# Forgetting attention by two pairs of heads at a time, its tail in another order, five moves in the order of the latent attention, and shifted buffers

## The chip, the cores and the metric

The kernel runs on one core of one Trainium2 chip. A core has a matrix engine (TensorE, PE), a vector engine (VectorE, DVE), a scalar engine (ScalarE, ACT), a general engine (GpSimd, POOL) and SyncE (SP), whose queue issues the DMA transfers here. Engines run their own streams in order and wait for one another through semaphores. The metric is the device time of one execution in microseconds (us).

## What is computed

The reference is a trunk of two layers on 256 tokens of width 1024. Each layer is a half-step SwiGLU network (FFN, inner width 2816), a mixer, a second FFN and a gated input embedding, each followed by a layer norm over `ALPHA*x + delta`. The mixer of layer 0 is forgetting attention (FoX, 16 heads of 64), that of layer 1 latent attention (MLA, 16 heads of 128 + 64 rotary columns), whose shared keys and values come from the residual stream between the layers.

```python
def swiglu(x, w_in, w_out):
    h = x @ w_in
    gate, up = h[..., :D_FF], h[..., D_FF:]
    return (jax.nn.silu(gate) * up) @ w_out

def fox_mixer(x, w_in, b_f, w_o):
    h = x @ w_in                      # q, k, v and 16 forget gates
    ...
    cum = jnp.cumsum(jax.nn.log_sigmoid(f_logit), axis=1).transpose(0, 2, 1)
    s = jnp.einsum('bqhd,bkhd->bhqk', qb, k) * scale + cb[:, :, :, None] - cum[:, :, None, :]
    # causal softmax over k in blocks of 128 queries, times v, then @ w_o

def mla_mixer(x, w_dq, q_norm, w_uq, w_o, k_nope, k_rope, v, cos, sin):
    c_q = rms_norm(x @ w_dq, q_norm)
    q = jnp.einsum('bsc,chd->bshd', c_q, w_uq)
    s = (jnp.einsum('bqhd,bkhd->bhqk', qn, k_nope) + jnp.einsum('bqhr,bkr->bhqk', qr, k_rope)) * scale
    # causal softmax, times the shared v, then @ w_o
```

All is float32. The kernel writes each float32 operand as the sum of two float32r numbers, hi and lo, and each product as three matmuls: hi*hi, hi*lo, lo*hi.

## The kernel before

**Weights.** They stream through three `raw` buffers of 1 MB by DMAs on SP's queue. A class `Stream` cuts each group into units and splits every unit: ACT copies it to hi (`L193`, `L201`), DVE subtracts to get lo (`L194`, `L205`). A split goes to a home: ten slots `hl`, and four further buffers `ota`, `otb`, `qk` and `fs` while they are lent to it. An ordinary split issues both halves at once; `ahead` issues the ACT half alone, `later` the DVE half that is left, `split_now` is the two together, and `fill(n)` splits until the n next units are ready. `use` hands a unit to matmuls; `pump`, called between matmuls, splits when estimated times of the engines allow it, unless `hold` is set.

**Order.** A recorder runs the whole program once to learn the order in which units are used. Then the program runs for good under a manual schedule: each engine gets its instructions as the code writes them. In the FoX mixer this is a loop over pairs of heads, in the MLA mixer the table `ORDER`, whose words name steps: `gen` (keys and queries of a head), `QK`, `sm` (softmax), `div`, `T` (transposes of the probabilities P into PT), `AV`, `O h t` (output product of head h for half t of the tokens), and `f n`, `a` and `l` for `fill`, `ahead` and `later`.

**FoX.** Per pair j of heads: `gen_k` and `gen_q` are 24 matmuls each (`h<-xT,hl`, 128x256), evicted to hi and lo by ACT and DVE. `QK(j)` has 14 matmuls into two banks of `y`: two that lay down the sum of the gates (`y<-negc,sel`) and twelve of keys by queries (`y<-qk`), each on 64 of the 128 rows, one head on the upper, the other on the lower half. `softmax(j)` adds the mask and takes the least on DVE (`L1033`, ISA in the order), corrects it by the gates (`L1040`, `L1041`, tile `tt`), takes exponentials on ACT (`L1045`), reciprocals on DVE (`L1052`, tile `su`) and divides on POOL (`L1055`). `T(j)` transposes P in six matmuls (`L1070`, `L493`) and evicts to PT, `AV(j)` is six matmuls 512 wide, evicted into `ota` or `otb` (`L1096`, `L1099`), and O(k, t) is six matmuls that add up the output (`y<-hl,ota` or `otb`). A step of the loop runs, on PE, QK(j), gen_q(j+1), AV(j-1), gen_k(j+2), T(j).

PSUM has eight banks in named rings: `y` has four, `h` and `tr` two each.

**Shared keys and values.** They are produced inside the first FFN of layer 1 (`kv`), whose h products begin with the first half of the tokens; `XT(1)` transposes the second half into `xT`, evicted in turn by ACT (`L498`) and DVE (`L499`).

## Time and profile before

| what | us |
|---|---|
| median of 3 runs (lowest, highest) | 1075.26 (1074.89, 1076.74) |
| profiled execution | 1074.41 |
| its span | 1072.3 |
| busy PE, DVE, ACT, POOL | 1061.1, 721.2, 543.9, 60.0 |
| HBM traffic over the span | 185 GB/s |

The granted clock of TensorE was 0.999. Rows of a timeline give the start in us, the busy time, the engine, the line, the operation, `out<-in`, the rows and columns of TensorE used, the shape, the count of like instructions that follow each other, and in brackets the idle time of the engine just before with the instruction that ended it. The end of a matmul is modelled, and one matmul starts before the one ahead ends; so waits of PE are best read from start to start. Rows of groups give busy time, mean ns of one, and idle time of the engine just before them.

### The profile page before, as it was taken

How to read it: one execution, taken by the hardware profiler on the slowest of the kernel's cores; microseconds unless marked ns; L12 is line 12 of the kernel's file. 1: busy time of each engine (PE TensorE's matmuls, PEld its weight loads, DVE VectorE, ACT ScalarE, POOL GpSimd, SP SyncE). 2: the span in 40 equal slices, each digit the busy share in tenths (PEclk: the TensorE clock that was granted, in tenths of full speed). 3: DMA queues.
4: the chain of work that ended last, by engine and by line, in shares of the span. 5: the costliest groups of instructions: out<-in, count | busy, mean ns of one | idle time of the engine just before them, and what ended most of it. 6: DMA issues, size and time to landing. Idle time of an engine off the chain costs nothing.

```text
span 1072.3 us, 17527 instructions
## 1 busy us (share of the span) xinstructions
PE 1061.1 (99%) x7236; PEld 971.9 (91%) x7236; DVE 721.2 (67%) x1053; ACT 543.9 (51%) x805; POOL 60.0 (6%) x94
## 2 busy tenths in 40 slices
PE   9999999999999999999999999999999999999997
PEld 9989998999889999998899999989899789898986
DVE  6775545788897545548966454578887886454566
ACT  6654433667645434444555453436675466354431
POOL 0000000223200000000320000000000000000000
PEclk9999999999999999999999999999999999999999
DMA  7886642543348655354477554423334568555502
GB/s 281 342 294 224 233 160 96 200 177 119 124 176 298 231 192 189 142 201 150 175 274 263 180 192 181 153 75 108 135 139 157 193 234 313 175 208 186 190 7 79
DMA packets 33091, 199.58 MB, mean 186 GB/s; under 512 B 3698, under 2 KB 5490, under 8 KB 12148
## 3 DMA queue, kind: packets, MB, share of 16 engines
q1 hardware_dynamic: 33012, 198.47, 51.5%
q8 instruction: 57, 0.93, 0.3%
q14 instruction: 22, 0.18, 0.1%
HBM read 197.40 MB, written 1.05 MB: 185 GB/s over the span
## 4 chain that ended last, share of the span: by engine, by line
PE 88%; DVE 7%; ACT 2%; issue 1%; POOL 1%; DMA 0%; DVEq 0%; SPq 0%; POOLq 0%; ACTq 0%
PE y L489 32%; PE h L489 31%; PE tr L489 22%; DVE hl L194 2%; PE tr L493 2%; ACT P L1434 1%; DVE PT L499 1%; ACT hl L193 0%; DVE tr L1429 0%; DVE x L569 0%; DVE hl L205 0%; PE h L493 0%; DVE qk L499 0%; DVE x L550 0%; DVE st L551 0%
## 5 line engine op out<-in xcount | busy, mean ns | idle before, releaser
L194 DVE TENSOR_TENSOR hl<-raw,hl 128x1024 fp32r<-128x1024 f32 (+3 forms) x263 | 309.2, 1194 | 148.3 <-ACT hl L193 147.4
L193 ACT ACTIVATE hl<-raw 128x1024 fp32r<-128x1024 f32 (+3 forms) x263 | 266.1, 1032 | 185.3 <-PE y L489 97.0
L489 PE MATMUL h<-xT,hl 128*128 128x256 f32 x1560 | 187.1, 279 | 0.3 <-DVE hl L233 0.2
L489 PE MATMUL y<-hl,g 128*128 128x512 f32 x792 | 185.7, 390 | 0.0
L489 PEld LDWEIGHTS h<-xT,hl 128*128 128x128 f32 x1560 | 182.8, 189 | 2.2 <-ACT xT L498 0.6
L489 PE MATMUL tr<-xT,hl 128*128 128x256 f32 x1512 | 176.6, 277 | 0.0
L489 PEld LDWEIGHTS tr<-xT,hl 128*128 128x128 f32 x1512 | 174.2, 188 | 0.5
L489 PEld LDWEIGHTS y<-hl,g 128*128 128x128 f32 x792 | 147.5, 188 | 29.8
L489 PE MATMUL h<-hl,xT 128*128 128x512 f32 (+2 forms) x300 | 67.8, 374 | 0.4 <-DVE xT L499 0.4
L489 PE MATMUL y<-hl,xT 128*128 128x512 f32 (+3 forms) x348 | 64.2, 334 | 0.0
L489 PEld LDWEIGHTS h<-hl,xT 128*128 128x128 f32 x300 | 53.2, 188 | 10.7 <-DVE xT L499 0.9
L489 PEld LDWEIGHTS y<-hl,xT 128*128 128x128 f32 x348 | 53.5, 188 | 6.3 <-ACT xT L498 0.4
L561 POOL TENSOR_TENSOR rs<-ve,mhalf 128x1 f32<-128x1 f32 x16 | 15.1, 942 | 627.9 <-DVE ve L560 627.9
L499 DVE TENSOR_TENSOR g<-P,g 128x512 fp32r<-128x512 f32 x38 | 26.3, 692 | 26.5 <-ACT g L498 26.5
L489 PE MATMUL y<-hl,otb 128*128 128x512 f32 x168 | 43.1, 397 | 0.2 <-DVE otb L1099 0.2
L498 ACT ACTIVATE xT<-tr 128x512 fp32r<-128x512 f32 x28 | 16.2, 597 | 48.2 <-PE tr L493 48.2
L498 ACT ACTIVATE g<-P 128x512 fp32r<-128x512 f32 x38 | 24.0, 632 | 32.8 <-DVE P L678 32.8
L194 DVE TENSOR_TENSOR otb<-raw,otb 128x1024 fp32r<-128x1024 f32 (+1 forms) x21 | 25.3, 1204 | 17.5 <-ACT otb L193 17.5
L194 DVE TENSOR_TENSOR qk<-raw,qk 128x1024 fp32r<-128x1024 f32 (+2 forms) x22 | 26.6, 1210 | 15.0 <-ACT qk L193 15.0
L489 PEld LDWEIGHTS y<-hl,otb 128*128 128x128 f32 x168 | 30.1, 188 | 6.1 <-DVE otb L1099 0.6
L193 ACT ACTIVATE otb<-raw 128x1024 fp32r<-128x1024 f32 (+1 forms) x21 | 21.8, 1039 | 19.7 <-PE y L489 10.8
L677 ACT ACTIVATE P<-tr 128x512 f32<-128x512 f32 x20 | 12.0, 599 | 38.0 <-PE tr L489 38.0
(264 smaller groups left out, 1420.4 us busy)
## 6 DMA issues: line engine op xcount, KB each, us to landing
raw<-in_ffn_in_dram SPq DMA_DIRECT2D x85, 1024.0 KB, 5.0
raw<-in_ffn_out_dram SPq DMA_DIRECT2D x44, 1024.0 KB, 4.9
raw<-in_pg_dram SPq DMA_DIRECT2D x8, 1024.0 KB, 4.8
raw<-in_mo_dram SPq DMA_DIRECT2D x8, 1024.0 KB, 4.7
raw<-in_kq_dram SPq DMA_DIRECT2D x8, 640.0 KB, 4.0
gb<-in_ln_g_dram SPq DMA_DIRECT2D x8, 512.0 KB, 5.8
gb<-in_ln_b_dram SPq DMA_DIRECT2D x8, 512.0 KB, 6.7
raw<-in_fk_dram SPq DMA_DIRECT2D x4, 1024.0 KB, 5.0
```

The source lines that it names most:

```text
L193: nc.scalar.activation(hi, src, AF.Copy)
L194: nc.vector.tensor_tensor(lo, src, hi.bitcast(F32), op=ALU.subtract)
L489: self.nc.tensor.matmul(out, lhsT, rhs, start=start, stop=stop)
L493: self.nc.tensor.transpose(out, in_, self.ident)
L498: self.nc.scalar.activation(hi, src, AF.Copy)
L499: self.nc.vector.tensor_tensor(lo, src, hi.bitcast(F32), op=ALU.subtract)
L561: nc.gpsimd.tensor_tensor(rs, ve, self.mhalf, op=ALU.pow)
L677: nc.scalar.activation(gt, ps[0], AF.Silu)
L1434: nc.scalar.activation(P[:, c0:c1], b[:, c0:c1], AF.Exp, bias=nm[:, q : q + 1], scale=-1.0, accum_out=su[:, q : q + 1],)
```

## The change

**The FoX loop takes two pairs of heads at a time.** Two QK blocks follow one another and fill all four `y` banks. `softmax` falls into `least` (DVE), `exps` (ACT) and `divide` (DVE and POOL), issued at different places. The correction by the gates and the reciprocals are made for both heads of a pair at once (128x4). AV goes into a bank of `h`, AV(5) into `tr`. Generation of the second pair, `gen_k(1)` and `gen_q(1)`, stands ahead of the transposes of the gates. Three `split_now` stand in the second half of a pair of pairs, two of them back to back.

On PE, the step of pair 1 in the loop before (`hl_...` are weight units, `g_...` the values):

```order
L489 MATMUL y<-negc,sel 128x384 x2
L489 MATMUL y<-qk 128x128 x2
L489 MATMUL y<-qk 128x256 x2
L489 MATMUL y<-qk 128x128 x2
L489 MATMUL y<-qk 128x256 x2
L489 MATMUL y<-qk 128x128 x2
L489 MATMUL y<-qk 128x256 x2
L489 MATMUL h<-xT,hl_2108 128x256 x24
L489 MATMUL y<-PT,g_1954 128x512 x3
L489 MATMUL y<-PT,g_2156 128x2x128 x3
L489 MATMUL h<-xT,hl_2082 128x256 x24
L1070 MATMUL tr<-ident,P 128x128 x4
```

And in the loop of the change, from the last matmuls of QK 2 on:

```order
L490 MATMUL y<-qk 128x256 x2
L490 MATMUL y<-negc,sel 128x384 x2
L490 MATMUL y<-qk 128x128 x2
L490 MATMUL y<-qk 128x256 x2
L490 MATMUL y<-qk 128x128 x2
L490 MATMUL y<-qk 128x256 x2
L490 MATMUL y<-qk 128x128 x2
L490 MATMUL y<-qk 128x256 x2
L490 MATMUL h<-PT,g_1956 128x512 x3
L490 MATMUL h<-PT,g_2158 128x2x128 x3
L490 MATMUL h<-xT,hl_2155 128x256 x24
L490 MATMUL h<-xT,hl_2232 128x256 x24
```

The next QK block follows the first directly, and AV of the pair before stands behind both, where a generation (24 matmuls) stood between QK and AV.

On DVE, the end of one step before, from the reciprocals of pair 1 (two rows in one) to PT:

```order
L1052 RECIPROCAL su<-su 128x2 x2
L205 TENSOR_TENSOR hl_2373<-raw,hl_2373 128x1024
L499 TENSOR_TENSOR qk<-h,qk 128x256
L1099 TENSOR_TENSOR ota<-y,ota 64x256 x2
L205 TENSOR_TENSOR fs<-raw,fs 128x1024
L499 TENSOR_TENSOR qk<-h,qk 128x256
L499 TENSOR_TENSOR PT<-tr,PT 128x512
L499 TENSOR_TENSOR PT<-tr,PT 128x256
```

And for pairs 2 and 3 in the change, from the reciprocals of pair 2 (the first row) and of pair 3 to PT of pair 2:

```order
L1071 RECIPROCAL su<-su 128x4
L206 TENSOR_TENSOR hl_2588<-raw,hl_2588 128x1024
L500 TENSOR_TENSOR qk<-h,qk 128x256
L1071 RECIPROCAL su<-su 128x4
L206 TENSOR_TENSOR hl_2669<-raw,hl_2669 128x1024
L206 TENSOR_TENSOR hl_2674<-raw,hl_2674 128x1024
L500 TENSOR_TENSOR qk<-h,qk 128x256
L500 TENSOR_TENSOR PT<-tr,PT 128x512
L500 TENSOR_TENSOR PT<-tr,PT 128x256
```

Where one split followed both reciprocals, one now follows that of the first pair, and two in a row that of the second.

**The FoX tail** runs QK 6, QK 7, AV 5, O 0 to O 4 of the first half of the tokens, T 6, O 5, the matmuls of AV 6, T 7, the evictions of AV 6, O 0 of the second half, AV 7, O 6, O 1 of the second half, O 7. Before, O 6 stood ahead of AV 7. SP issues three more weight loads ahead of those of the norm's factors (`gb`), and one split moves behind the layer norm.

**`S.stop`** names a unit that `pump` may not split: in the `kv` FFN, unit 2 of the third product, until `XT(1)` has been issued. On DVE the split now stands behind the two evictions into `xT`.

**The table of the MLA mixer** has four places changed. `l` and a fill move from ahead of QK 4 and softmax 4 to behind them; O 5 0 moves ahead of AV 6; AV 12 moves ahead of gen 15; and a fill ahead of softmax 15 is dropped, with one `f 2` for two `f 1` behind it. On DVE, around softmax 15 before (ISA is the masked least, `nm` its result):

```order
L499 TENSOR_TENSOR PT<-tr,PT 128x384
L194 TENSOR_TENSOR hl_8425<-raw,hl_8425 128x1024
L1429 ISA tr,nm<-tr,mask 128x128
L1429 ISA nm 128x1
L1429 ISA tr,nm<-tr,mask 128x256
L1429 ISA nm 128x1
L1443 RECIPROCAL su<-su 128x2
L1446 TENSOR_SCALAR P<-P,su 128x128
L1446 TENSOR_SCALAR P<-P,su 128x256
```

And in the change:

```order
L500 TENSOR_TENSOR PT<-tr,PT 128x384
L1466 ISA tr,nm<-tr,mask 128x128
L1466 ISA nm 128x1
L1466 ISA tr,nm<-tr,mask 128x256
L1466 ISA nm 128x1
L195 TENSOR_TENSOR hl_8416<-raw,hl_8416 128x1024
L1480 RECIPROCAL su<-su 128x2
L1483 TENSOR_SCALAR P<-P,su 128x128
L1483 TENSOR_SCALAR P<-P,su 128x256
```

The split has moved from ahead of the softmax to between its least and its reciprocal.

**Buffers.** Two unused tiles of 192 and 64 bytes per partition stand around the first `gb`, so that it and all that is allocated behind it lie 192 or 256 bytes higher; slices of the shared keys in `fs` start 192 and 256 bytes later.

```diff
@@ -54,23 +54,23 @@
...
-    "l", "O 1 0", "O 1 1", "AV 2", "f 4", "a", "f 3", "gen 5", "T 3", "f 4", "l", "QK 4", "sm 4", "f 1", "f 1",
+    "l", "O 1 0", "O 1 1", "AV 2", "f 4", "a", "f 3", "gen 5", "T 3", "f 4", "QK 4", "sm 4", "l", "f 1",
...
-    "QK 7", "sm 7", "f 4", "gen 8", "div 7 0", "zs 1 1", "l", "zU 0 1", "f 4", "gen 9", "f 4", "AV 6", "f 2",
-    "O 5 0", "zU 1 0", "QK 8", "a", "T 7", "sm 8", "f 1", "O 5 1", "div 8 0", "f 3", "O 6 0", "f 4", "f 1",
+    "QK 7", "sm 7", "f 4", "gen 8", "div 7 0", "zs 1 1", "l", "zU 0 1", "f 4", "gen 9", "f 4", "O 5 0", "AV 6",
+    "f 2", "zU 1 0", "QK 8", "a", "T 7", "sm 8", "f 1", "O 5 1", "div 8 0", "f 3", "O 6 0", "f 4", "f 1",
...
@@ -138,6 +138,7 @@
         self.hold = False
         self.rest = None
         self.at = 0
+        self.stop = None
 
     def load(self, n=NRAW):
         while self.loaded < len(self.groups) and self.loaded < self.done + n:
@@ -284,7 +285,7 @@
 
     def pump(self):
 
-        if self.ready == len(self.order) or not self.slots or self.hold:
+        if self.ready == len(self.order) or not self.slots or self.hold or self.order[self.ready] == self.stop:
             return
         arrival = self.arrives.get(group_of(self.order[self.ready]), 1e12)
         if arrival <= self.pe_t + 500 and max(self.act_t, self.dve_t) <= self.pe_t + SLACK_NS:
@@ -538,7 +539,12 @@
                 self.S.pump()
 
     def load_gb(self, li, i):
+        first = (li, i) == (0, 0)
+        if first:
+            self.tl([128, 48], F32, "gap0", 1)
         self.gb = self.tl([128, 2, D], F32, "gb", 1)
+        if first:
+            self.tl([128, 16], F32, "gap1", 1)
         if not self.rec:
             self.dma(self.gb[:, 0, :], pbcast(self.a["ln_g"][li, i], D))
             self.dma(self.gb[:, 1, :], pbcast(self.a["ln_b"][li, i], D))
@@ -702,7 +708,13 @@
             first()
         else:
             H(0, 0, sweeps=SW_H00)
-            H(1, 0, HAT, lambda: self.XT(1), SW_H10)
+            S.stop = ("win", li, which, 2, 0) if kv else None
+
+            def other():
+                self.XT(1)
+                S.stop = None
+
+            H(1, 0, HAT, other, SW_H10)
             if kv:
                 self.kv_down(1)
             H(0, 1, sweeps=SW_H01)
@@ -989,17 +1001,17 @@
         qk = self.own([128, 2, 2, 512], F32R, "qk")
         OT = [self.own([128, 4, 2, 256], F32R, tag) for tag in ("ota", "otb")]
 
-        def gen(j, key, c0, at={}, hold=False):
+        def gen(j, key, c0, hold):
             ps = self.bank("h")
-            ws((key, j), ps[:, 0:256], at, hold)
+            ws((key, j), ps[:, 0:256], hold=hold)
             o = qk[:, j % 2]
             self.parts(o[:, 0, c0 : c0 + 256], o[:, 1, c0 : c0 + 256], ps[:, 0:256])
 
         def gen_k(j):
-            gen(j, "fk", 256, {0: S.split_now} if j >= 2 else {}, j >= 2)
+            gen(j, "fk", 256, j >= 2)
 
         def gen_q(j):
-            gen(j, "fq", 0, {}, j >= 2)
+            gen(j, "fq", 0, j >= 2)
 
         def QK(j, ring):
             sb = [self.bank(ring) for _ in range(2)]
@@ -1020,14 +1032,12 @@
                         )
             st[j] = sb
 
-        def softmax(j):
+        seg = ((0, 128), (128, 384))
+
+        def least(j):
             sb = st[j]
             nm = self.tl([128, 4], F32, "nm", 2)
             tt = self.tl([128, 4], F32, "tt", 2)
-            su = self.tl([128, 4], F32, "su", 2)
-            pair = self.tl([128, 768], F32, "P", 2)
-            P = [pair[:, 384 * s : 384 * s + 384] for s in range(2)]
-            seg = ((0, 128), (128, 384))
             for s in range(2):
                 for q, (c0, c1) in enumerate(seg):
                     nc.vector.tensor_tensor_reduce(
@@ -1035,10 +1045,17 @@
                         op0=ALU.add, op1=ALU.min, scale=-0.125, scalar=3.0e38,
                         accum_out=nm[:, 2 * s + q : 2 * s + q + 1],
                     )
-                c2 = cq[:, 2 * j + s, :]
-                i = slice(2 * s, 2 * s + 2)
-                nc.vector.tensor_tensor(tt[:, i], nm[:, i], c2, op=ALU.subtract)
-                nc.vector.tensor_tensor(tt[:, i], tt[:, i], c2, op=ALU.add)
+            c2 = cq[:, 2 * j : 2 * j + 2, :].rearrange("p h t -> p (h t)")
+            nc.vector.tensor_tensor(tt, nm, c2, op=ALU.subtract)
+            nc.vector.tensor_tensor(tt, tt, c2, op=ALU.add)
+            self.S.busy(dve=1400)
+            st[j] = sb, tt
+
+        def exps(j):
+            sb, tt = st[j]
+            su = self.tl([128, 4], F32, "su", 2)
+            pair = self.tl([128, 768], F32, "P", 2)
+            P = [pair[:, 384 * s : 384 * s + 384] for s in range(2)]
             for s in range(2):
                 for q, (c0, c1) in enumerate(seg):
                     i = 2 * s + q
@@ -1046,19 +1063,18 @@
                         P[s][:, c0:c1], sb[s][:, c0:c1], AF.Exp, bias=tt[:, i : i + 1], scale=-1.0,
                         accum_out=su[:, i : i + 1],
                     )
-            self.S.busy(act=1800, dve=1400)
-
-            def divide(s):
-                nc.vector.reciprocal(su[:, 2 * s : 2 * s + 2], su[:, 2 * s : 2 * s + 2])
+            self.S.busy(act=1800)
+            st[j] = P, su
+
+        def divide(j):
+            P, su = st[j]
+            nc.vector.reciprocal(su, su)
+            for s in range(2):
                 for q, (c0, c1) in enumerate(seg):
                     i = 2 * s + q
                     nc.gpsimd.tensor_scalar(
                         P[s][:, c0:c1], P[s][:, c0:c1], su[:, i : i + 1], 1.0, op0=ALU.mult, op1=ALU.mult
                     )
-
-            divide(0)
-            divide(1)
-            S.later()
             st[j] = P
 
         def T(j):
@@ -1077,9 +1093,9 @@
             self.parts(o[:, 0, 512:768], o[:, 1, 512:768], b1[:, 0:256])
             PT[j] = o
 
-        def AV(j):
+        def AV(j, what=None):
             o = PT.pop(j)
-            ps = self.bank("y" if j < 6 else "tr")
+            ps = self.bank("h" if j != 5 else "tr")
             n, c = j // 4, 128 * (j % 4)
             strided = ps.rearrange("p (s c) -> p s c", s=2)[:, :, 128:256]
             for m, (i, jj) in enumerate(((0, 0), (0, 1), (1, 0))):
@@ -1089,6 +1105,8 @@
                     strided, v[1, n][:, i, c : c + 128],
                     o[:, jj, 512:768].rearrange("p (s c) -> p s c", s=2), False, m == 2,
                 )
+            if what:
+                what()
             ot = OT[j // 4][:, j % 4]
             self.S.busy(act=700, dve=600)
             for s in range(2):
@@ -1116,41 +1134,60 @@
                     lambda i: w[:, i, 512 * n : 512 * n + 512], k == 0, k == 7,
                 )
 
-        for j in range(8):
-            if j == 2:
+        gen_k(1)
+        gen_q(1)
+        self.flush()
+        gates_transpose()
+        S.lend("fs")
+        S.hold = True
+        for a in range(0, 6, 2):
+            if a == 2:
                 self.load_gb(li, 1)
-            S.hold = j >= 1
-            if j < 7:
-                gen_k(j + 1)
-            else:
-                O(0, 0)
-                O(1, 0)
-            if j == 0:
-                self.flush()
-                gates_transpose()
-                S.lend("fs")
-            if j >= 1:
-                T(j - 1)
-                if j < 7:
-                    S.ahead()
-            QK(j, "y" if j < 7 else "h")
-            softmax(j)
-            if j < 7:
-                gen_q(j + 1)
-            else:
-                O(2, 0)
-                S.split_now()
-                O(3, 0)
-            if j >= 1:
-                AV(j - 1)
+            QK(a, "y")
+            QK(a + 1, "y")
+            least(a)
+            if a:
+                AV(a - 1)
+            exps(a)
+            S.ahead()
+            least(a + 1)
+            gen_k(a + 2)
+            exps(a + 1)
+            divide(a)
+            S.later()
+            gen_q(a + 2)
+            divide(a + 1)
+            S.split_now()
+            S.split_now()
+            gen_k(a + 3)
+            T(a)
+            S.split_now()
+            gen_q(a + 3)
+            AV(a)
+            T(a + 1)
+        QK(6, "y")
+        QK(7, "h")
+        least(6)
+        AV(5)
+        exps(6)
+        least(7)
+        S.lend("qk")
+        exps(7)
+        divide(6)
+        divide(7)
+        for k in range(2):
+            O(k, 0)
+        S.split_now()
+        for k in range(2, 5):
+            O(k, 0)
+        T(6)
+        S.split_now()
+        O(5, 0)
+        AV(6, lambda: T(7))
+        O(0, 1)
         S.hold = False
-        S.lend("qk")
-        O(4, 0)
-        O(5, 0)
-        T(7)
+        AV(7)
         O(6, 0)
-        O(0, 1)
-        AV(7)
         O(1, 1)
         O(7, 0)
         self.ln(0, y[0], ALPHA, LN_EPS)
@@ -1205,8 +1242,8 @@
     def kv_transpose_rope(self):
         nc = self.nc
         kvt = self.kvt = self.own([128, 2048], F32R, "fs")
-        self.ckv = kvt[:, 0:1024].rearrange("p (i c) -> p i c", i=2)
-        self.kr = kvt[:, 1024:1792].rearrange("p (i c) -> p i c", i=3)
+        self.ckv = kvt[:, 48:1072].rearrange("p (i c) -> p i c", i=2)
+        self.kr = kvt[:, 1088:1856].rearrange("p (i c) -> p i c", i=3)
         b = self.bank("tr")
         for t in range(2):
             self.transpose(b[:, 128 * t : 128 * t + 128], self.kvtok[:, t, 256:384])
```

10 rows, old and new, of the table ORDER are left out of this document.

## The prediction

> **What bounds the kernel now.** I read the page first, then the timeline of TensorE (PE) for what follows another late, then the engines that feed it at those places.
>
> ```profile
> PE 1061.1 (99%) x7236; PEld 971.9 (91%) x7236; DVE 721.2 (67%) x1053; ACT 543.9 (51%) x805; POOL 60.0 (6%) x94
> 228.38:262.55 34.17, 34.17 (x298) 32.47 (x298) 29.05 (x88) 24.16 (x65) 10.18 (x16) 1.00 0.42 155
> ```
>
> PE is busy 1061.1 of 1072.3 us. The second row is the windows view over four steps of the forgetting-attention loop (PE, PEld, DVE, ACT, POOL busy): PE has no gap in 34.17 us, DVE is at 29.05, 85%. The change keeps the 7236 matmuls. So there are two sources of gain alone: matmuls that start closer together, and the short holes where PE waits for DVE. One step of the loop, then part of a QK block by itself:
>
> ```profile
> 222.06 5.73 PE L489 MATMUL h<-xT,hl 128*128 128x256 f32 x48
> 227.63 0.60 PE L1070 MATMUL tr<-ident,P 128*128 128x128 f32 x4
> ...
> 228.38 0.45 PE L489 MATMUL y<-negc,sel 64*128 64x384 f32 x2
> 228.67 0.85 PE L489 MATMUL y<-qk 64*128 64x128 f32 x12
> 229.44 3.01 PE L489 MATMUL h<-xT,hl 128*128 128x256 f32 x24
> 232.30 1.21 PE L489 MATMUL y<-PT,g 128*128 128x512 f32 x6
> 233.34 3.00 PE L489 MATMUL h<-xT,hl 128*128 128x256 f32 x24
> 236.18 0.60 PE L1070 MATMUL tr<-ident,P 128*128 128x128 f32 x4
> 236.62 0.38 PE L493 MATMUL tr<-ident,P 128*128 128x128 f32 x2
> 236.93 0.44 PE L489 MATMUL y<-negc,sel 64*128 64x384 f32 x2
> ...
> 246.03 0.40 PE L489 MATMUL y<-qk 64*128 64x256 f32 x4
> 246.21 0.39 PE L489 MATMUL y<-qk 64*128 64x128 f32 x4
> 246.27 0.33 PE L489 MATMUL y<-qk 64*128 64x256 f32 x2
> 246.53 0.39 PE L489 MATMUL h<-xT,hl 128*128 128x256 f32 x1
> ```
>
> A step is 236.93 - 228.38 = 8.55 us, start to start. The QK block works on half the rows (64*128), and each change between it and full-row work costs. Going in: four transposes take 0.44 (236.18 to 236.62), two take 0.31 instead of 0.22 when QK follows, +0.09. Going out: 24 matmuls behind a QK take 2.86 (229.44 to 232.30), while 48 took 5.57 (222.06 to 227.63), so 24 without it take 2.71, +0.15. The last pair of 256-wide QK matmuls takes 0.26 (246.27 to 246.53), the one before 0.18 (246.03 to 246.21), +0.08. Together 0.32 us for each lone block.
>
> **1. QK in pairs.** Eight lone blocks become four of two; four times in and out go: 4 x 0.32 = -1.28. Against it: 24 generating matmuls behind AV take 2.84 (233.34 to 236.18), 0.13 more than 2.71. Five groups stand behind AV before; in the new order it is three each for the pairs at 2 and 4, six, +0.13. The inner block's first two matmuls (0.29, 228.38 to 228.67) may also start faster: at the pace of the 0.18 for 256 columns, 384 would take 0.27, so almost nothing is to be had there. If the last-pair and exit costs turn out to belong to every block, only the entry is saved, 4 x 0.09 = 0.36. I take -1.15, between -0.2 and -1.4. The merged tt operations, reciprocals and the split softmax are DVE work beside a busy PE: nothing, as long as DVE's 15% of slack covers it.
>
> **2. The tail.** Here one hole of PE:
>
> ```profile
> 294.00 1.20 PE L489 MATMUL y<-hl,otb 128*128 128x512 f32 x4 [0.19 <-DVE otb L1099]
> ```
>
> The idle in the bracket counts from the modelled end of the matmul before. Undisturbed matmuls start 0.16 before that end (229.44 + 3.01 = 232.45 against 232.30), so a wait seen start to start is the bracket plus 0.16: here 0.35. O of pair 7 waits for the DVE eviction of AV 7. Before, O 1 alone stands between AV 7 and O 7; in the change O 6 and O 1 do, six matmuls more. I take the hole as gone, -0.4 with its restart, between 0 and -0.5. T(7)'s evictions, now issued behind AV 6's matmuls, and the three fo loads that SP issues ahead of gb have several us of O before their readers: nothing. One split fewer is made before the layer norm and one more behind it, with other work of PE in front of its reader: nothing, at most the 1.2 us of a DVE split (row in part 5). AV now shares the banks of the generation; each is emptied behind a block of 24 matmuls, so I see no wait in that.
>
> **3. S.stop in the shared-KV stage.**
>
> ```profile
> 533.79 1.73 PE L489 MATMUL h<-hl,xT 128*128 128x320 f32 x10 [0.39 <-DVE xT L499]
> 529.44 3.69 DVE L194 TENSOR_TENSOR hl<-raw,hl 128x1024 fp32r<-128x1024 f32 x3
> 533.06 1.28 DVE L499 TENSOR_TENSOR xT<-tr,xT 128x512 fp32r<-128x512 f32 x2
> ```
>
> PE waits 0.39 + 0.16 = 0.55 for the xT parts, which DVE starts right when three splits end at 533.13. With the third behind xT they come 1.2 us earlier, more than the wait. The held split's reader comes after another group of matmuls. -0.55, between -0.2 (the wait turns to ACT's half of xT) and -0.65.
>
> **4. The table of the latent attention.**
>
> ```profile
> 765.88 0.61 PE L493 MATMUL tr<-ident,P 128*128 128x128 f32 x3 [0.16 <-DVE P L1446]
> 762.26 1.21 DVE L205 TENSOR_TENSOR hl<-raw,hl 128x1024 fp32r<-128x1024 f32 x1
> 763.39 0.29 DVE L1429 CUSTOM_DVE_ANT_0 tr<-tr,mask 128x128 f32<-128x128 f32 x1
> ...
> 783.92 1.24 PE L489 MATMUL h<-gb,hl 128*128 128x256 f32 x9
> 785.27 0.91 PE L489 MATMUL h<-PT,g 128*128 128x256 f32 x6
> 786.01 1.59 PE L489 MATMUL y<-hl,otb 128*128 128x512 f32 x6
> ...
> 825.60 0.51 PE L493 MATMUL tr<-ident,P 128*128 128x128 f32 x3
> 826.23 1.82 PE L489 MATMUL y<-hl,ota 128*128 128x512 f32 x6
> ...
> 836.81 0.61 PE L493 MATMUL tr<-ident,P 128*128 128x128 f32 x3 [0.38 <-DVE P L1446]
> 832.23 0.56 DVE L499 TENSOR_TENSOR PT<-tr,PT 128x384 fp32r<-128x384 f32 x1 [0.72 <-ACT PT L498]
> 833.18 1.22 DVE L194 TENSOR_TENSOR hl<-raw,hl 128x1024 fp32r<-128x1024 f32 x1 [0.39 <-ACT hl L193]
> 834.32 0.29 DVE L1429 CUSTOM_DVE_ANT_0 tr<-tr,mask 128x128 f32<-128x128 f32 x1
> 836.17 0.17 DVE L1443 RECIPROCAL su<-su 128x2 f32<-128x2 f32 x1 [0.98 <-ACT P L1434]
> ```
>
> T 4 waits 0.16 + 0.16 = 0.32 behind a softmax that DVE begins at 763.39 because a split runs first; with "l" behind "sm 4" the softmax starts up to 1.2 earlier: -0.32. AV 6 waits 785.27 - 783.92 - (1.24 - 0.16) = 0.27; O 5 0, a block like the six at 786.01 (1.59 - 0.16 = 1.43 us), now stands ahead of it: -0.27. O 12 0 waits 826.23 - 825.60 - (0.51 - 0.16) = 0.28 for AV 12's eviction, and its six take longer by the second half; AV 12 one generation earlier saves up to 0.6, of which AV 13, now nearer to its own PT, gives back about half: -0.3. The fourth move is a loss by its place: the split at 833.18 leaves the front of softmax 15, but its ACT half now follows the exponentials and its DVE half stands ahead of the reciprocal. From softmax to reciprocal it is 836.17 - 834.32 = 1.85 us; begun at 832.8, where DVE ends the PT row, the exponentials are done at 834.6, ACT's half of a split (1.03, row below) at 835.7, DVE's 1.22 at 836.9. The reciprocal comes 0.7 late, and T 15, which waits already (0.38 + 0.16), with it; DVE's evictions behind it slip too, so AV 15 gives little back. I take +0.6, between 0 and +1.1 (ACT's and DVE's halves half covered, or nothing of the earlier start realised). Sum of the table -0.3, between -1.2 and +0.6.
>
> **5. Homes.**
>
> ```profile
> L194 DVE TENSOR_TENSOR hl<-raw,hl 128x1024 fp32r<-128x1024 f32 (+3 forms) x263 | 309.2, 1194 | 148.3 <-ACT hl L193 147.4
> L193 ACT ACTIVATE hl<-raw 128x1024 fp32r<-128x1024 f32 (+3 forms) x263 | 266.1, 1032 | 185.3 <-PE y L489 97.0
> L194 DVE TENSOR_TENSOR qk<-raw,qk 128x1024 fp32r<-128x1024 f32 (+2 forms) x22 | 26.6, 1210 | 15.0 <-ACT qk L193 15.0
> ```
>
> The buffers move by 192, 64 or 256 bytes. The same split takes 1194 ns into the ten hl homes and 1210 into the qk home, quite another place, so I cost the move at nothing. If these 16 ns were an effect of the address and fell on each of the 285 splits of the two rows, it would be 4.6 us of DVE, with either sign, and DVE is mostly off the path.
> The Trainium skill says, in SBUF — State Buffer, Specifications (TRN2), that cachelines are 16 bytes; all three shifts are whole lines. No run here shows it.
>
> **Sum.** -1.15 - 0.4 - 0.55 - 0.3 = -2.4. The profiled execution, 1074.41 (span 1072.3 and 2.1 around it), would become 1072.0. The median of the three runs, 1075.26, lies 0.85 above it; I forecast against the median: **1072.9 us**. About 0.2% (2.15 us) is what a measurement tells from no change, so the edge of faster is 1073.1.
>
> **Rivals.** (a) *POOL is shut out, in every pair.* The rows:
>
> ```profile
> 258.18 0.82 POOL L1055 TENSOR_SCALAR P<-P,su 128x128 f32<-128x128 f32 x2 [5.73 <-DVE su L1052]
> 259.27 1.72 POOL L1055 TENSOR_SCALAR P<-P,su 128x128 f32<-128x128 f32 x2 [0.27 <-DVE su L1052]
> ...
> 259.10 1.20 DVE L205 TENSOR_TENSOR hl<-raw,hl 128x1024 fp32r<-128x1024 f32 x1
> ...
> 529.70 2.37 POOL L1193 TENSOR_SCALAR PT<-PT,rs 128x256 f32<-128x256 f32 x1
> ```
>
> Two POOL divisions take 0.82, but 1.72 when a DVE split runs beside them; at 529.70 one took 2.37 through the splits at 529.44. The change puts two splits back to back right behind the reciprocal of pair a+1, while POOL is still at pair a's four divisions. From the reciprocal they need 0.27 (the bracket at 259.27), 1.72 for the first two beside a split and 0.41 (0.82 / 2) for the third: the fourth starts after 2.4 us. The second reciprocal, and the splits behind it, come one generation later, after 2.71 to 2.84. The point that decides is this margin of 0.3 to 0.4; it is less at the first pair, whose softmax has no AV in front of the generation that follows, so that its reciprocal comes late. A fourth division that misses it ends 1.9 us late (2.37 - 0.48), and T(a) on PE with it. In three pairs +5.7, so -2.4 + 5.7 = +3.3, 1078.6, slower; chance 18%. For it: DVE is 85% full, so reciprocals drift late. Against it: in two of the three pairs nothing in these rows takes up the margin.
> The Trainium skill's SBUF — State Buffer, Who interferes with whom, speaks against the change: a DVE instruction with two SBUF inputs and a GpSimd one that reads SBUF hold a shared pair of ports exclusively, and the loser blocks for the whole instruction. By that rule, this trace agrees (1.72 against 0.82).
> (b) *Only the first pair misses:* -2.4 + 1.9 = -0.5, 1074.8, no change that can be told; 20%.
> (c) *QK costs stay with each block,* (entry only saved, and the six slow groups): -0.2 in place of -1.15: -1.45, 1073.8, no change; 14%.
> The forecast's case has 48%: as it lies only 0.2 below the edge, 3 of these may end in no change, while (c) may end below the edge by as much if the table gives more. So faster 0.47, no change 0.34 (20 + 14), slower 0.19.
>
> **Range.** Low: every term at its far end, -1.4 - 0.5 - 0.65 - 1.2 = -3.75, 1071.5, and 0.9, the distance between the profiled run and the median, below it: 1070.6. High: (a) in two pairs, -2.4 + 3.8 = +1.4, and the same 0.9: 1077.5; (a) in full lies outside. The forecast's case alone: 1071.5 to 1073.4.
>
> **What would show it.** In the changed profile: QK 6 to QK 7 and the pairs as 24 + 4 narrow matmuls without a full-row one between; a pair's period near 2 x 8.55 - 0.3 = 16.8 us; no releaser at T 4, the kv group, O 7 or AV 6; T 15 with a bracket larger than 0.38. What would make it wrong: T(0), T(2) or T(4) with a bracket that names POOL; AV(a-1) waiting for DVE's PT; or all stages longer at once, which would be the homes.

## The result, and the profile after

The changed kernel takes 1070.53 us (median of 5, 1070.12 to 1071.00); the kernel before, on the same chip, 1074.89 (1074.74 to 1076.74). The ratio is 0.9951, with a 95% interval of 0.994 to 0.9961: half a per cent less, clear of the noise. I had forecast 1072.9 with a range from 1070.6. The direction was right. The gain was 4.4 us where I had 2.4, and the time lies just below the range.

The profiled executions took 1074.41 (span 1072.3) and 1070.54 (span 1068.8). Since TensorE (PE) is the bound in both, the start of the same matmul in both traces tells what each stretch gained. Rows of PE's timeline before, then after: a matmul ahead of the FoX loop, the first long group of the FFN behind it, the first transposes ahead of the MLA mixer, the first transposes behind it.

```profile
207.78 1.54 PE L489 MATMUL y<-otb,xT 128*128 128x512 f32 x6
...
321.64 5.66 PE L489 MATMUL h<-hl,xT 128*128 128x512 f32 x24
...
706.43 0.60 PE L493 MATMUL tr<-ident,x 128*128 128x128 f32 x4
...
849.35 0.60 PE L493 MATMUL tr<-ident,x 128*128 128x128 f32 x4
```

```profile
208.08 1.53 PE L490 MATMUL y<-otb,xT 128*128 128x512 f32 x6
...
320.07 5.66 PE L490 MATMUL h<-hl,xT 128*128 128x512 f32 x24
...
704.22 0.60 PE L494 MATMUL tr<-ident,x 128*128 128x128 f32 x4
...
845.85 0.60 PE L494 MATMUL tr<-ident,x 128*128 128x128 f32 x4
```

| stretch | after minus before at its end | gain | predicted |
|---|---|---|---|
| up to the FoX loop | +0.30 | | 0 |
| FoX, loop and tail | -1.57 | 1.87 | 1.55 |
| FFN, input embedding, FFN with the shared keys | -2.21 | 0.64 | 0.55 |
| MLA mixer | -3.50 | 1.29 | 0.3 |

The three stretches gain 3.80 us. The +0.30 at the start is no part of the change (see the last section). The two profiled executions differ by 3.87: 3.80 - 0.30 and 0.37 outside the span, for the time is 2.11 above the span before and 1.74 after. That last part belongs to the change: all traced kernels with the new FoX code, in all their executions, have 1.73 to 1.90 around the span, and all with the old one 2.06 to 2.24, some 0.33 more. Where it goes is open, as the trace holds the span alone. So the change is worth some 4.1 us; the rest of the 4.4 is within the executions' spread.

The FoX loop after, on PE: two QK blocks, AV, three generations, and the start of the next round.

```profile
239.43 0.44 PE L490 MATMUL y<-negc,sel 64*128 64x384 f32 x2
239.71 0.85 PE L490 MATMUL y<-qk 64*128 64x128 f32 x12
240.41 0.33 PE L490 MATMUL y<-negc,sel 64*128 64x384 f32 x2
240.57 0.85 PE L490 MATMUL y<-qk 64*128 64x128 f32 x12
241.36 1.32 PE L490 MATMUL h<-PT,g 128*128 128x512 f32 x6
242.52 8.64 PE L490 MATMUL h<-xT,hl 128*128 128x256 f32 x72
...
256.19 0.44 PE L490 MATMUL y<-negc,sel 64*128 64x384 f32 x2
```

From one pair of blocks to the next it is 256.19 - 239.43 = 16.76 us, two steps before took 2 x 8.55 = 17.10. There is no bracket in these rows. The second block's first two matmuls take 0.16 to 0.17 (240.41 to 240.57) where the first block's take 0.28.

The fourth pair, QK 6 and QK 7, does not gain this. QK 7 goes into the two banks of `h`, and AV 4 has just been in one of them. PE, then DVE:

```profile
272.64 0.44 PE L490 MATMUL y<-negc,sel 64*128 64x384 f32 x2
...
273.61 0.69 PE L490 MATMUL h<-negc,sel 64*128 64x384 f32 x2
273.90 1.09 PE L490 MATMUL h<-qk 64*128 64x128 f32 x12
274.93 1.34 PE L490 MATMUL tr<-PT,g 128*128 128x512 f32 x6
```

```profile
272.89 0.86 DVE L1117 TENSOR_TENSOR otb<-h,otb 64x256 fp32r<-64x256 f32 x2 [1.00 <-ACT otb L1114]
```

DVE empties AV 4's bank until 273.75. Only then do the second head's matmuls start, 0.29 behind the first head's instead of together with them. From the first block to AV the pair takes 2.29 us (272.64 to 274.93) instead of 1.93 (239.43 to 241.36). No bracket shows this wait of 0.36, since the other head keeps PE busy.

In the MLA mixer after, the holes at T 4 and AV 6 are gone, and T 15 waits longer:

```profile
762.13 1.23 PE L490 MATMUL h<-gb,hl 128*128 128x256 f32 x9
763.19 0.49 PE L494 MATMUL tr<-ident,P 128*128 128x128 f32 x3
...
780.99 1.18 PE L490 MATMUL h<-gb,hl 128*128 128x256 f32 x9
782.01 1.54 PE L490 MATMUL y<-hl,otb 128*128 128x512 f32 x6
783.38 0.80 PE L490 MATMUL h<-PT,g 128*128 128x256 f32 x6
...
822.34 1.64 PE L490 MATMUL y<-hl,ota 128*128 128x512 f32 x6
823.82 1.11 PE L490 MATMUL h<-PT,g 128*128 128x256 f32 x6
...
833.51 0.61 PE L494 MATMUL tr<-ident,P 128*128 128x128 f32 x3 [0.84 <-DVE P L1483]
...
835.35 1.05 PE L490 MATMUL h<-PT,g 128*128 128x256 f32 x6
```

T 15's wait is 0.84 + 0.16 = 1.00, against 0.54 before. O 12 0 (822.34) doesn't wait, AV 13 behind it takes 1.11 in place of 0.80. The group in front of AV 6 has changed too: nine matmuls on `gb` now take 1.18, before 1.24. Nothing in the order explains that; the experiments do.

On POOL, the divisions of pairs 0 and 1, each row as the timeline at its own place gives it, and DVE beside them:

```profile
231.01 1.16 POOL L1075 TENSOR_SCALAR P<-P,su 128x128 f32<-128x128 f32 x1 [12.88 <-DVE su L1071]
232.95 0.48 POOL L1075 TENSOR_SCALAR P<-P,su 128x256 f32<-128x256 f32 x1
233.40 2.39 POOL L1075 TENSOR_SCALAR P<-P,su 128x128 f32<-128x128 f32 x1
```

```profile
232.54 0.17 DVE L1071 RECIPROCAL su<-su 128x4 f32<-128x4 f32 x1
233.14 1.35 DVE L206 TENSOR_TENSOR hl<-raw,hl 128x1024 fp32r<-128x1024 f32 x1 [0.44 <-ACT hl L202]
234.42 1.21 DVE L206 TENSOR_TENSOR fs<-raw,fs 128x1024 fp32r<-128x1024 f32 x1
```

My rival (a) is here, one division later than I feared. The fourth division starts at 232.95, the first of the two splits at 233.14, so the fifth (of pair 1) is shut out for 2.39 us, and pair 1 has time: T 1 begins at 238.69. The margin was 0.19 us, and the split owes it to its wait of 0.44 for ACT, which I had not counted.

### The profile page after: what moved, and what is told of

It reads as the page before. It is cut to its first block, busy times and chain, and to the rows that moved or that the text cites. A ratio compares the mean times of both kernels' runs of the same rounds, so it can differ in the third digit from the quotient of the medians.

```text
span 1068.8 us, 17497 instructions
## 1 busy us (share of the span) xinstructions
PE 1057.0 (99%) x7236; PEld 969.8 (91%) x7236; DVE 717.7 (67%) x1029; ACT 541.8 (51%) x805; POOL 64.6 (6%) x94
## 3 DMA queue, kind: packets, MB, share of 16 engines
HBM read 197.40 MB, written 1.05 MB: 186 GB/s over the span
## 4 chain that ended last, share of the span: by engine, by line
PE 96%; DVE 1%; issue 1%; ACT 1%; POOL 0%; DMA 0%; SPq 0%; DVEq 0%; POOLq 0%; ACTq 0%
PE y L490 36%; PE h L490 35%; PE tr L490 23%; PE tr L494 2%; DMA raw<-in_w_dram 0%; PE h L494 0%; PE tr L1086 0%; ACT hl L194 0%; DVE x L575 0%; POOL fs L957 0%; POOL fs L950 0%; SPq L360 0%; SPq L476 0%; DVE hl L195 0%; ACT P L1471 0%
## 5 line engine op out<-in xcount | busy, mean ns | idle before, releaser
L490 PE MATMUL h<-xT,hl 128*128 128x256 f32 x1560 | 184.8, 278 | 1.5 <-ACT hl L232 1.2
L490 PE MATMUL y<-hl,g 128*128 128x512 f32 x780 | 182.3, 390 | 0.0
L684 DVE TENSOR_TENSOR P<-P,tr 128x512 f32<-128x512 f32 x20 | 13.8, 688 | 30.0 <-PE tr L490 15.2
```

What stands on the lines that cost most here:

```text
L490: self.nc.tensor.matmul(out, lhsT, rhs, start=start, stop=stop)
L684: nc.vector.tensor_tensor(gt, gt, ps[1], op=ALU.mult)
```

## The experiments

Twelve kernels were run. Differences of a few tenths of a us are below what the times tell, so each verdict rests on the stretch of the trace that the edit touches, taken as in the table above, and the medians stand beside it. Where nothing in it was changed, the stretch of the MLA mixer repeats within 0.1 us, and that of the shared keys within 0.02. The FoX stretch varies by 0.3 between kernels with the same order, all of it in the generation ahead of QK 0: its first 48 matmuls go at 113 or 118 ns, and then PE waits 0.3 to 0.6 us for DVE to empty a bank of `h`, before as well as after. From QK 0 on it takes 95.96 to 96.05; so e3 and e12 are compared from there.

| run | median us | ratio to before, 95% interval | in its stretch |
|---|---|---|---|
| e1, change without homes | 1071.07 | 0.9962 (0.995 to 0.9975) | MLA +0.40 to the change |
| e2, fill put back | 1070.71 | 0.9957 (0.9945 to 0.997) | MLA -0.23 to the change |
| e3, break between QK blocks | 1073.09 | 0.998 (0.9971 to 0.9989) | FoX +1.3 to the change |
| e4, before with homes | 1074.44 | 0.9991 (0.9982 to 1.0) | MLA -0.22 to before |
| e5, gb by 256 bytes | 1070.50 | 0.9957 (0.9942 to 0.9972) | MLA +0.2 to the change |
| e6, gb by 128 bytes | 1071.39 | 0.9962 (0.995 to 0.9973) | MLA +0.3 to the change |
| e7, before with FoX | 1072.50 | 0.998 (0.997 to 0.999) | FoX -1.69 to before |
| e8, before with table | 1074.94 | 1.0001 (0.9991 to 1.001) | MLA -0.80 to before |
| e9, change without stop | 1072.50 | 0.9973 (0.9964 to 0.9983) | shared keys +0.67 to the change |
| e10, division ahead of fills | 1070.94 | 0.9954 (0.9941 to 0.9966) | MLA -0.6 to the change |
| e11, one split behind T 15 | 1072.54 | 0.9966 (0.9952 to 0.9979) | MLA +0.39, FFN behind it +0.63 to the change |
| e12, split ahead of reciprocal | 1072.11 | 0.9978 (0.9967 to 0.9989) | FoX +1.5 to the change |

**e1 and e4: the homes, taken away and alone.**

```diff
-        if first:
-            self.tl([128, 48], F32, "gap0", 1)
...
-        if first:
-            self.tl([128, 16], F32, "gap1", 1)
...
-        self.ckv = kvt[:, 48:1072].rearrange("p (i c) -> p i c", i=2)
-        self.kr = kvt[:, 1088:1856].rearrange("p (i c) -> p i c", i=3)
+        self.ckv = kvt[:, 0:1024].rearrange("p (i c) -> p i c", i=2)
+        self.kr = kvt[:, 1024:1792].rearrange("p (i c) -> p i c", i=3)
```

> The change with its buffers put back (no unused tiles around gb, slices of the shared keys at their old places); the order on every engine is that of the change. Theory A, that the homes cost nothing, as I predicted: the time of the change, 1070.5 within 0.5 us, and the matmuls h<-gb,hl of the latent attention at the median spacing of the change, 117 ns. Theory B, that the place of gb and of the shared keys sets how close the matmuls that read them can start: h<-gb,hl back at 120 ns and h<-fs,hl at 120, and 0.4 to 0.7 us more, all of it between 700 and 840 us of the span.

For e4 the lines that e1 takes out of the change are added to the kernel before.

> The kernel before with the shifted buffers alone; the order on every engine is that of before. Theory A, homes cost nothing: the time of before within 0.5 us. Theory B: h<-gb,hl at 117 ns instead of 120 and h<-fs,hl at 118, 0.4 to 0.7 us less, as far as the wait of an engine behind them does not take it back. If the time falls by 1 us or more, other stages gain by the homes too and the measured difference that the trace does not show lies there.

One group of nine on `gb`, PE's timeline of e1, then of e4:

```profile
781.37 1.24 PE L490 MATMUL h<-gb,hl 128*128 128x256 f32 x9
```

```profile
784.10 1.18 PE L489 MATMUL h<-gb,hl 128*128 128x256 f32 x9
```

Without the homes the group takes 1.24 again, with them alone 1.18. Start to start, the median of the 144 matmuls on `gb` is 120 ns in before and e1, and 117 in the change and e4. For those on `fs` it is 119 without the shift and 118 with it. Theory B holds, and the homes are worth 0.40 us in the MLA mixer of the change. In that of before it is 0.22, less than expected, since waits behind these groups take part of it back. At the foot of e4's expectation stood a gain elsewhere; its trace shows none.

**e5 and e6: which distance.** `gb` moves by 256 or 128 bytes instead of 192; every other buffer stays.

```diff
-            self.tl([128, 48], F32, "gap0", 1)
+            self.tl([128, 64], F32, "gap0", 1)
...
-        if first:
-            self.tl([128, 16], F32, "gap1", 1)
```

> The change with gb 256 bytes above its old place instead of 192; all other buffers and the order on every engine as in the change. In the two kernels traced so far the matmuls h<-gb,hl start 120 ns apart where the address read as the moving operand (gb) and that of the weights (hl) are equal modulo 256, and 113 or 118 ns apart where they differ by 192. Theory: the distance modulo 256 decides: back to 120 ns, and about 0.4 us more than the change between 720 and 830 us. Rival: any other place does, the old one was bad by itself: 113 to 118 ns, the time of the change.

```diff
-            self.tl([128, 48], F32, "gap0", 1)
+            self.tl([128, 32], F32, "gap0", 1)
...
-            self.tl([128, 16], F32, "gap1", 1)
+            self.tl([128, 32], F32, "gap1", 1)
```

> The change with gb 128 bytes above its old place; the rest as in the change. Distance to the weights is 128 modulo 256. If only equal addresses modulo 256 collide: 113 or 118 ns for h<-gb,hl, the time of the change. If the collision repeats every 128 bytes: 120 ns and 0.4 us more.

```profile
781.57 1.22 PE L490 MATMUL h<-gb,hl 128*128 128x256 f32 x9
```

```profile
782.10 1.23 PE L490 MATMUL h<-gb,hl 128*128 128x256 f32 x9
```

Both are slow again: a median of 119 ns, single matmuls from 112 to 123, and 0.2 and 0.3 us in the mixer where I expected 0.4. So the rival "any other place does" falls, and so does "only equal addresses modulo 256": 128 is as bad as 256. What the runs bear out is that distances of 0, 128 and 256 bytes (modulo 256: 0 or 128) between the moving operand and the weights cost 2 to 3 ns a matmul, by the medians, against 192. The remainder modulo 256 is not all of it: 0 gives mostly 120 and 256 a mixture. Why stays open, and so does at which distances the cost repeats.

**e7, e8 and e9: the parts alone.** e7 is the kernel before with the new FoX loop and tail; e8 with the new table; e9 is the change without the held split; its edit:

```diff
-            S.stop = ("win", li, which, 2, 0) if kv else None
+            S.stop = None
```

> The kernel before with the new loop and tail of forgetting attention alone (old table, old homes, no held split). By the trace of the change this part is worth 1.85 us between 220 and 303 us, 3 x 0.35 of it from the pairs' steps: I expect 1.7 to 2.0 us less in that stretch and the waits of before everywhere else (T 4 0.32, AV 6 0.27, T 15 0.55, the group of the shared keys 0.55). My prediction had 1.55 for it.

> The kernel before with the new table of the latent attention alone (old homes). Taking from the 1.3 us that the change gains between 700 and 845 us the 0.45 that the homes give by the run without them: 0.8 to 0.9 us less in that stretch, of which T 4 0.4, AV 6 0.35, O 12 and AV 13 0.3, and T 15 with AV 15 0.2 more. My prediction had 0.3 in sum. If it is 0.3, the homes and the table do not add up and part of the gain belongs to both.

> The change without the held split in the first FFN of layer 1. By the trace the change gains 0.66 us at the group of the shared keys; I expect that hole back (0.55 start to start, releaser DVE xT) and 0.6 to 0.7 us more between 528 and 542 us, nothing elsewhere.

e7 gains 1.69 us in its stretch, e8 0.80, and e9 loses 0.67, with the hole back in its place. The group in e9, then in the change, where it has no bracket:

```profile
533.16 1.73 PE L490 MATMUL h<-hl,xT 128*128 128x320 f32 x10 [0.40 <-DVE xT L500]
```

```profile
533.14 1.04 PE L490 MATMUL h<-otb,xT 128*128 128x320 f32 x6
```

The parts add up within the 0.3 of the FoX stretch: 1.69 + 0.67 + 0.80 + 0.40 = 3.56, against 3.80. In e8, T 4 gives some 0.45 and AV 6 some 0.4, and the last two moves about cancel (AV 12's gives 0.2 there and 0.27 in the trace of the change, and T 15 with AV 15 takes 0.25 back). Its ratio, 1.0001, does not resolve 0.8 us; that it gains rests on the trace alone.

**e3: what a pair of QK blocks saves.**

```diff
             QK(a, "y")
+            self.transpose(self.bank("h")[:, 0:128], self.ident)
             QK(a + 1, "y")
```

> The change with one full-row transpose of the identity (128 columns, nothing reads it) between the two QK blocks of the pairs 0, 2 and 4. Theory: what a pair saves is the switch between half-row and full-row work, so each break costs the transpose (0.11) and the switch back and forth, 0.3 to 0.45: 1.2 to 1.7 us in the three pairs, and the first two matmuls of the second block take 0.28 again instead of 0.17. Rival: the gain of the pairs came from the softmax and the splits standing elsewhere, not from the switch: 0.33 us, three transposes.

```profile
241.06 0.44 PE L490 MATMUL y<-negc,sel 64*128 64x384 f32 x2
241.34 0.85 PE L490 MATMUL y<-qk 64*128 64x128 f32 x12
242.12 0.33 PE L494 MATMUL h<-ident 128*128 128x128 f32 x1
242.38 0.44 PE L490 MATMUL y<-negc,sel 64*128 64x384 f32 x2
242.66 0.86 PE L490 MATMUL y<-qk 64*128 64x128 f32 x12
243.45 1.32 PE L490 MATMUL h<-PT,g 128*128 128x512 f32 x6
```

From the first block to AV it is 2.39 us (241.06 to 243.45), in the change 1.93 (239.43 to 241.36): +0.46, of which 0.11 is the transpose and 0.35 the switch. The inner block's first two take 0.28 again. That is the switch, and 3 x 0.46 = 1.4 accounts for the 1.3 of the stretch; the rival's 0.33 is too little. The three pairs that the kernel's loop makes are thus worth some 3 x 0.35 = 1.05 us. The fourth, of the tail, takes 2.29 as it is, no less than a broken pair without its transpose (2.39 - 0.11 = 2.28): its wait for the bank costs what the missing switch saves.

**e12: POOL shut out.**

```diff
-            divide(a)
             S.later()
+            divide(a)
```

> The change with the split that follows the first reciprocal of each two pairs moved ahead of it, so that POOL's four divisions start later against the two splits that follow the second reciprocal; PE, ACT, POOL and SP keep their order. In the change POOL's fourth division of the first pair starts at 232.95, 249.26 and 266.01, and the first of the two splits at 233.14, 249.73 and 266.33: margins of 0.19, 0.47 and 0.32. With the reciprocal behind the split they shrink by 0.32 to 0.41 (1.19 later, but the first division is not shut out for 1.16): about -0.13, 0.07 and -0.1. Rival of my prediction, shut out by splits: the fourth division of pairs 0 and 4 takes about 2.4 us instead of 0.48, PE gets a hole of 1.3 to 1.6 at T 0 and T 4 each, T 2 is on the edge, and the time rises by 2.6 to 4.5 us. If being shut out costs POOL alone: no hole, the time of the change.

```profile
232.61 2.50 POOL L1075 TENSOR_SCALAR P<-P,su 128x256 f32<-128x256 f32 x1
```

```profile
235.17 0.33 PE L1086 MATMUL tr<-ident,P 128*128 128x128 f32 x1 [1.11 <-POOL P L1075]
...
268.11 0.83 PE L1086 MATMUL tr<-ident,P 128*128 128x128 f32 x4
```

The fourth division of pair 0 takes 2.50 us, and T 0 gets a hole of 1.11 + 0.16 = 1.27 with POOL as its releaser. T 2 is spared. At T 4 the division takes 1.55 only, since it got in behind the first of the two splits, and four transposes take 0.67 (268.11 to the next row's 268.78) in place of 0.44. In five such meetings of the two traces POOL waited for both splits, in this one for one; why is open. The stretch loses 1.5, not the 2.6 to 4.5 that I wrote, but the mechanism is as the rival had it. The change passes it by 0.19 us.

**e2, e10 and e11: the place of a split around softmax 15.** e2 restores the old fills, e10 puts the division ahead of both, e11 also moves one split behind T 15.

```diff
-    ... "QK 15", "T 14", "lend", "O 13 0", "sm 15",
-    "f 2", "div 15 0", "l", "AV 14", ...
+    ... "QK 15", "T 14", "f 3", "lend", "O 13 0", "sm 15",
+    "f 1", "f 1", "div 15 0", "l", "AV 14", ...
```

> The change with the fill ahead of softmax 15 put back, and two fills of one behind it. By the trace of the change T 15 waits 1.00 us where it waited 0.55, and AV 15 behind it 0.26 where it waited 0.39: I expect T 15 back at about 0.55 and 0.2 to 0.3 us less in all. If AV 15 gives everything back: the time of the change.

```diff
-    "f 2", "div 15 0", "l", "AV 14", "O 7 1", "f 3", "O 8 1",
+    "div 15 0", "f 2", "l", "AV 14", "O 7 1", "f 3", "O 8 1",
```

> The change with the division of softmax 15 ahead of the two fills instead of behind them, so that no split stands between its least and its reciprocal. If T 15 waits only for that split's two halves: the hole of 1.00 us at T 15 is gone altogether (the reciprocal comes at about 2.0 us behind the least, before PE is there), AV 15 waits up to 0.5 instead of 0.26 since PE comes earlier to the same PT, and 0.6 to 1.0 us less in all. If the exponentials on ACT bound it: a hole of 0.3 to 0.5 is left.

```diff
-    "f 2", "div 15 0", "l", "AV 14", "O 7 1", "f 3", "O 8 1",
+    "div 15 0", "f 1", "l", "AV 14", "O 7 1", "O 8 1",
```

> As the run before, and one of the two splits behind softmax 15 goes behind T 15, so that PT of head 15 is evicted before it. If AV 15 waits for DVE's queue: its wait goes too, 0.2 to 0.4 us less than the run before, unless the output products of the last heads then wait for their weights (releaser DVE hl), which costs as much.

PE's timeline in e2, e10 and e11:

```profile
833.53 0.61 PE L494 MATMUL tr<-ident,P 128*128 128x128 f32 x3 [0.39 <-DVE P L1483]
...
835.87 0.79 PE L490 MATMUL h<-PT,g 128*128 128x256 f32 x5 [0.21 <-DVE PT L500]
```

```profile
833.52 0.49 PE L494 MATMUL tr<-ident,P 128*128 128x128 f32 x3
...
835.98 0.79 PE L490 MATMUL h<-PT,g 128*128 128x256 f32 x5 [0.45 <-DVE PT L500]
```

```profile
839.36 0.73 PE L490 MATMUL y<-hl,fs 128*128 128x512 f32 x2 [0.30 <-ACT fs L499]
841.07 1.19 PE L490 MATMUL y<-hl,fs 128*128 128x512 f32 x4 [0.97 <-DVE fs L500]
```

e2 gives back 0.23 us, as expected. e10 takes T 15's hole away altogether; AV 15's grows to 0.45 + 0.16 = 0.61; net 0.6 better than the change. e11 takes both away, but then O 15 0 waits 0.30 and 0.97 for the eviction of AV 15, queued behind the splits on ACT and DVE, and the FFN behind waits 0.51 for ACT's half of a split: against the change a loss of 0.39 in the mixer and 0.63 behind it, where I had expected a gain on e10. e10 beats the change by its trace; its time, 1070.94 (from 1069.52 to 1071.44), cannot be told from 1070.53.

## Why the prediction was right or wrong

**QK in pairs: right in kind, wrong in the terms.** The switch costs what I read, about 0.35 a block with entry and exit, but it was saved three times and not four. "I see no wait in that", of AV in the banks of the generation, failed: QK 7 follows AV 4 into them without a block of generation between, and its wait of 0.36 takes the fourth saving back. Still the loop gained more than the -1.15: from QK 0 to QK 6 it takes 48.61 us (224.03 to 272.64) for 50.09 before (221.00 to 271.09), 1.48 less. Of this 1.05 are the three switches; some of the rest are generation groups at the faster pace, and the remainder I can't assign. That the FoX stretch came out at 1.87 for my 1.55 is thus in part luck. Two more sentences failed. "Almost nothing is to be had" from the inner block's first two matmuls: they take 0.16 to 0.17 instead of 0.28; a pace for 256 columns was no guide for two 384-wide matmuls on the two halves. And "six, +0.13" for groups behind AV: the generation groups behind the pairs at 2 run at 118 ns, those behind the pairs at 4 at 113, in the traces of the change, e1, e2 and e3 alike, so 3 groups are slow and not 6. Why, I can't say.

**Tail and shared keys: right.** The hole at O 7 is gone: its matmuls, in a row of 18 from 295.97 on, have no bracket. The one of the shared keys was 0.67 by e9, where I had 0.55: the start of the matmuls behind a wait costs some 0.1 more than the wait.

**The table: right in the places, mis-sized in the sum.** I had -0.3, e8 measured -0.80; by size this is the largest miss. Two moves were worth some 0.45 and 0.4, where I had 0.32 and 0.27, since again I counted the wait and not the restart: AV 6 took 0.74 behind its wait (785.27 to 786.01), without it 0.64 (783.38 to 784.02, where the next row begins). The fourth move is a loss, as I said, but of 0.25 instead of 0.6: T 15 waits 0.46 longer, and AV 15 "gives little back" was wrong, it gave back 0.2, because its PT was waited for anyway.

**Homes: the step that failed.** "I cost the move at nothing", because splits on DVE and ACT take the same time in all homes. That looked at the engines that write to the homes. The reader that matters is PE, which reads two buffers at once, and it was in the trace of before: the matmuls on `gb` start 120 ns apart, other 256-wide ones 113 or 118. e1 and e4 show 0.2 to 0.4 us. Without the homes, the change takes 1071.07 (e1), within my range. In that step the Trainium skill's SBUF — State Buffer, Specifications (TRN2), gave me lines of 16 bytes and whole lines moved; the measurement says that whole lines can still matter.

**The sum.** 1.55 + 0.55 + 0.3 became 1.87 + 0.64 + 1.29 = 3.80. I also kept the 2.1 around the span, which fell by 0.33. That my low end of the terms, -3.75, is near 3.80 is luck: it has 1.2 for the table and nothing for the homes. On the fast side I had given 0.9 for the executions' spread. The 0.33 took a part of it; the kernel before, whose median is 1074.89 by five executions and was 1075.26 by three, another 0.37; and the rest was not enough.

**Rival (a)** did not decide, but not for the reason that I had named. The second reciprocal comes 1.90 to 2.17 us behind the first, not 2.71 to 2.84; the margins of 0.19 to 0.47 that are left come from the splits' wait of 0.44 for ACT. So a margin of about the size that I had is luck. e12 shows that the rival is real and 0.19 us away. The Trainium skill's SBUF — State Buffer, Who interferes with whom, is borne out: an instruction of POOL that meets two splits takes 2.39 to 2.50 us instead of 0.37 to 0.48 (once 1.55, in e12), and, issued without a split beside it, its usual time.

## What to carry to other kernels

Where one engine is busy 99%, read the pace of its instructions from start to start and not its idle time: much of the gain here lay in matmuls that began closer together, by fewer switches between half-row and full-row work and by other distances between buffers. A wait can hide in the same way, as at QK 7. A wait on that engine is worth the wait and some 0.1 us of restart. And when splits are packed on the vector engine, look at what the general engine has in flight: here 0.19 us decided over 1.3.

## What the runs showed of the hardware

**The distance between two buffers.** Matmuls 128x256 with the moving operand in `gb` and weights in `hl` start 120 ns apart (the median) at a distance of 0, 119 (112 to 123) with `gb` shifted by 128 or 256 bytes, and 113 or 118 with a shift of 192.

**Two paces.** The same 96 matmuls of the first FFN (before that, nothing has changed) took 10.88 us from start to start in one execution and 11.38 in another. PE's timeline of the change, and of e10, whose instructions are the same there:

```profile
17.11 11.04 PE L490 MATMUL tr<-xT,hl 128*128 128x256 f32 x96
27.99 5.60 PE L490 MATMUL h<-xT,hl 128*128 128x256 f32 x48
```

```profile
16.15 11.54 PE L490 MATMUL tr<-xT,hl 128*128 128x256 f32 x96
27.53 5.82 PE L490 MATMUL h<-xT,hl 128*128 128x256 f32 x48
```

That is 113 and 118 ns each, with no wait in between. At which pace a long run goes differs between executions in the first 140 us, and the first of these 96 matmuls, behind the first weights, starts between 16.15 and 19.86 us. So the traces of kernels whose order is the same up to there reach the matmul ahead of the FoX loop between 207.30 and 210.81 us. That this makes most of the spread of one kernel's times, 1074.1 to 1078.8 for the kernel before, is likely and not shown, since one execution of each kernel is traced. What chooses the pace is open.
